# Rotating a matrix by 90 degrees: a staging grid of 63 places, three output buffers, and a late chunk

## The chip, the cores and the metric

The kernel runs on one core of one Trainium2 chip. The time is the device time of one execution in microseconds, and the number that counts is the median of several runs. A profile is one more execution, taken by the hardware profiler.

## The reference

```
def reference(x, k):            # x: 8192 x 8192 float32, k = 1
    return np.rot90(x, k)       # out[8191 - j, i] = x[i, j]
```

Every element is read once and written once: 268.44 MB in and 268.44 MB out. No arithmetic is done.

## The kernel before

**Tiles.** The matrix is cut into 16 tiles of 1024 rows by 4096 columns (`tiles`, line 71). A tile has T = 8 row tiles t of 128 rows, and its columns have 8 chunks c of C = 512. `grid` (line 63) holds one whole tile on chip, 8 x 8 places of 512 floats in each of the 128 partitions.

**A rotation in two halves.** A row tile is loaded in one DMA of 2 MB (128 partitions by 4096 floats) into a buffer `a` (line 92, issued by SP). `reverse` (line 96, VectorE, DVE in the profile) copies it into its 8 places of the grid, with each block of 128 columns in reverse order. `store` makes one output: TensorE (PE) transposes 32 blocks of 128x128, those of one chunk of all 8 row tiles, into two PSUM tiles of 2048 floats (line 119). ScalarE (ACT) copies each half to the output buffer `ot` (line 135) and issues one DMA of 2 MB to `out` (line 137).

**One grid for two tiles.** Output i of tile m reads one column of places, and when its transposes are done those 8 places are free. Row tile i of tile m+1 goes into them. So even tiles lie in the grid as (t, c) and odd ones as (c, t) (`row_tile`, line 75, and `block`, line 79). The order written out by hand (lines 145 to 155) is: load and reverse all of tile 0; then for each m and i: load row tile i of tile m+1, store output i of tile m, reverse row tile i of tile m+1. The last tile is stored in eight outputs of half the rows and twice the columns.

**Buffers.** `a_pool` and `o_pool` have two buffers each, of 16 KB in a partition; the grid has 128 KB. During the loads of tile 0, when nothing is stored yet, every third and fourth load borrows an output buffer (line 87). In the last tile three of the outputs borrow a load buffer (line 152).

**Who waits for whom.** A load waits until the reversal of the row tile that had its buffer is done. The reversal of row tile i waits for its load and for the transposes of output i. The transposes wait for ACT to empty PSUM. ACT's copy waits for the transposes and for the landing of the store that had the output buffer. The first output of a tile needs the last row tile; there the transposes run row tile by row tile (`by_row`), so that the last comes last.

Of the kernel before, what the change touches and what calls it, by code (L numbers as in the profile page):

```python
# [2 lines left out]

# [5 lines left out]

P = 128  # L10
T = 8
R = T * P
W = 4096
C = W // T
F = 4096
FP = 2048


def whole_reads(nc):

    for fn in nc.m.functions:
        for block in fn.blocks:
            for n, ins in enumerate(block.instructions):
                if not isinstance(ins, mybir.InstDMACopy):
                    continue
                src = ins.ins[0]
                ap = [list(d) for d in src.ap]
                if len(ap) == 3 and ap[2][0] == 1 and ap[1][0] == ap[2][1]:
                    ap = [ap[0], [1, 1], [1, ap[1][1] * ap[2][1]]]
                    block.instructions[n] = copy.replace(  # L30
                        ins,
                        ins=[copy.replace(src, ap=ap)],
                        ant_dge_precooked=False,
                    )


@with_exitstack
def kernel(
    ctx: ExitStack,
    tc: tile.TileContext,  # L40
    x: bass.AP,
    k: bass.AP,
    out: bass.AP,
):

    nc = tc.nc
    assert k == 1, f"only k=1 supported, got {k}"
    nc.at_finalize(whole_reads)

    N, M = x.shape
    dt = x.dtype

    consts = ctx.enter_context(tc.tile_pool(name="consts", bufs=1))  # L60
    ident = consts.tile([P, P], dt)
    make_identity(nc, ident)
    grid = consts.tile([P, T, T, C], dt)

    a_pool = ctx.enter_context(tc.tile_pool(name="a_pool", bufs=2))
    o_pool = ctx.enter_context(tc.tile_pool(name="o_pool", bufs=2))
    psum_pool = ctx.enter_context(
        tc.tile_pool(name="psum", bufs=2, space=bass.MemoryType.PSUM)
    )

    tiles = [(r0, c0) for r0 in range(0, N, R) for c0 in range(0, M, W)]
    LAST = len(tiles) - 1
    H = T // 2

    def row_tile(m, t):

        return grid[:, t] if m % 2 == 0 else grid[:, :, t]

    def block(m, t, b):

        c, b = divmod(b, C // P)
        at = grid[:, t, c] if m % 2 == 0 else grid[:, c, t]
        return at[:, b * P : (b + 1) * P]

    def load(m, t):
        r0, c0 = tiles[m]
        if m == 0 and t % 4 >= 2:
            a = o_pool.tile([P, W], dt, tag="o")
        else:
            a = a_pool.tile([P, W], dt, tag="a")  # L90
        r0 += t * P
        nc.sync.dma_start(out=a[:], in_=x[r0 : r0 + P, c0 : c0 + W])  # L92
        return a

    def reverse(m, t, a):
        nc.vector.tensor_copy(  # L96
            out=row_tile(m, t).rearrange("r c (b m) -> r c b m", m=P),
            in_=a[:].rearrange("r (c b m) -> r c b m", c=T, m=P)[:, :, :, ::-1],
        )

    def store(m, rows, i, pool, by_row):

        r0, c0 = tiles[m]
        r0 += rows[0] * P
        n = len(rows) * P
        G = F // n
        PW = FP // n
        if pool is a_pool:
            ot = a_pool.tile([P, F], dt, tag="a")
        else:  # L110
            ot = o_pool.tile([P, F], dt, tag="o")
        o = ot[:].rearrange("m (g f) -> m g f", g=G)
        ps = []
        for h in range(2):
            pt = psum_pool.tile([P, FP], mybir.dt.float32, tag="ps")
            ps.append(pt[:].rearrange("m (g f) -> m g f", g=PW))

        def transposes(h, w, t):
            nc.tensor.transpose(  # L119
                ps[h][:, PW - 1 - w, t * P : (t + 1) * P],  # L120
                block(m, rows[t], i * G + h * PW + w),
                ident,
            )

        if by_row:
            for t in range(len(rows)):
                for h in range(2):
                    for w in range(PW):
                        transposes(h, w, t)
        for h in range(2):  # L130
            if not by_row:
                for w in range(PW):
                    for t in range(len(rows)):
                        transposes(h, w, t)
            nc.scalar.copy(o[:, G - PW - h * PW : G - h * PW, :], ps[h])  # L135
        top = M - c0 - (i + 1) * G * P
        nc.scalar.dma_start(  # L137
            out=out[top : top + G * P, r0 : r0 + n].rearrange(
                "(g m) f -> m g f", g=G
            ),  # L140
            in_=o,
        )

    every = list(range(T))
    for t in every:
        reverse(0, t, load(0, t))
    for m in range(LAST):
        for i in every:
            a = load(m + 1, i)
            store(m, every, i, o_pool, i == 0)  # L150
            reverse(m + 1, i, a)
    pools = [o_pool, o_pool] + [a_pool, o_pool] * 3
    for i, pool in enumerate(pools):
        rows = every[i // H * H :][:H]
        store(LAST, rows, i % H, pool, False)


# [1 line left out]
_INS = ['x', 'k']  # L159
_OUTS = [((8192, 8192), 'float32')]  # L160

_NUMBERS = {'k': 1}


# [26 lines left out]
```

## Time and profile before

| | |
|---|---|
| three runs | 1267.73, 1269.55, 1270.55 us; median 1269.55 |
| the profiled execution | 1267.78 us, of which the span (first to last instruction) is 1265.9 us |
| DMA queue of the loads (q1), of the stores (q10) | 268.44 MB each; 49.7% and 50.0% of 16 engines' span |
| rate over the span | 424 GB/s |
| PE matmul | 721.7 us busy, 4096 instructions |
| ACT copies | 465.3 us busy, 256 of 1869 ns |
| DVE copies | 293.6 us busy, 128 of 2294 ns |
| a load, a store, from issue to landing (median) | 17.1 us, 15.9 us |
| what ends most of ACT's idle time | a store's landing: 733.5 us |
| what ends most of DVE's idle time | a load's landing: 717.5 us |

The profile page has the span in 40 slices with the busy share of each engine in tenths (9 is 90% or more) and the rate of the DMA engines, and the chain of work that ended last, followed back from the end. The trace answers further questions: the busy time of each engine in any stretch of the span (columns: stretch, its length, PE, PE's weight load, DVE, ACT and POOL busy with counts, the granted clock of PE, the mean busy share of the 16 DMA engines, GB/s), and instructions in order of time with the idle time before them and what ended it in square brackets. ACTq and SPq are the queues from which ACT and SP issue DMAs.

### The profile page before, as it was taken

The page shows a single profiled execution, that of the slowest core. Times are in us where ns is not written, and L with a number is a line of the kernel's source. Part 1 is how long each engine was busy: PE and PEld are TensorE (multiplying, and loading weights), DVE is VectorE, ACT ScalarE, POOL GpSimd, SP SyncE. Part 2 cuts the span into 40 slices and gives each one's busy share as a digit, 9 for nine tenths or more (in the row PEclk, how much of TensorE's full clock was granted, in tenths as well). Part 3 has the DMA queues.
Part 4 walks back from the last instruction along what each step waited for, and adds up shares of the span by engine and source line. Part 5 has one row for each costly group of instructions (what it writes and reads, how often), then busy time and mean ns, then how long its engine had stood idle before and what let it go on. Part 6 is the DMA issues. An engine that isn't in the chain of part 4 may idle for free.

```text
span 1265.9 us, 9281 instructions
## 1 busy us (share of the span) xinstructions
PE 721.7 (57%) x4096; PEld 683.4 (54%) x4096; DVE 293.6 (23%) x128; ACT 466.6 (37%) x257; POOL 0.7 (0%) x6
## 2 busy tenths in 40 slices
PE   1355665566556565565545655556565565565674
PEld 1355554556546554565545645556455564565574
DVE  3322222222222222222222222222222222222210
ACT  0243333433344333333343333433343333433364
POOL 0000000000000000000000000000000000000000
PEclk9977677676777868768687786877868768768687
DMA  9999999999999999999999999999999999999989
GB/s 398 428 427 426 427 429 430 430 428 429 428 430 430 429 429 429 428 430 428 429 429 429 430 428 429 428 429 427 427 429 428 429 427 426 429 427 428 429 361 375
DMA packets 36904, 537.48 MB, mean 425 GB/s; under 512 B 4096, under 2 KB 4096, under 8 KB 4096
## 3 DMA queue, kind: packets, MB, share of 16 engines
q10 hardware_dynamic: 18432, 268.44, 50.0%
q1 hardware_dynamic: 18432, 268.44, 49.7%
q8 instruction: 32, 0.52, 0.2%
q14 instruction: 8, 0.07, 0.0%
HBM read 268.44 MB, written 268.44 MB: 424 GB/s over the span
## 4 chain that ended last, share of the span: by engine, by line
DMA 78%; ACT 19%; issue 1%; DVE 0%; ACTq 0%; PE 0%; SPq 0%
DMA out_dram<-ot 75%; ACT ot L135 19%; DMA a<-in_x_dram 3%; DVE grid L96 0%; PE pt L119 0%; ACTq L137 0%; SPq L92 0%; ACTq L135 0%
## 5 line engine op out<-in xcount | busy, mean ns | idle before, releaser
L119 PE MATMUL pt<-ident,grid 128*128 128x128 f32 x4096 | 721.7, 358 | 528.2 <-ACT ot L135 491.2
L119 PEld LDWEIGHTS pt<-ident,grid 128*128 128x128 f32 x4096 | 683.4, 192 | 566.3 <-ACT ot L135 526.3
L135 ACT COPY ot<-pt 128x2048 f32<-128x2048 f32 x256 | 465.3, 1869 | 745.7 <-DMA out_dram<-ot 733.5
L96 DVE COPY grid<-a 128x4096 f32<-128x4096 f32 x128 | 293.6, 2294 | 920.7 <-DMA a<-in_x_dram 717.5
L135 ACT ACT_TABLE_LOAD x1 | 1.3, 1283 | 39.8 <-DVE grid L96 39.8
masks.py:199 POOL TENSOR_SCALAR_AFFINE_SELECT ident<-ident 128x128 f32<-128x128 f32 x1 | 0.3, 292 | 0.1
masks.py:197 POOL MEMSET ident<- 128x128 f32 x1 | 0.2, 204 | 0.3 <-POOLq L172 0.3
L172 POOL MEMSET const-bfloat16-1.0<- 128x1 bf16 x1 | 0.1, 101 | 0.0
L172 POOL MEMSET const-uint8-127<- 128x1 uint8 x1 | 0.1, 101 | 0.0
L172 POOL MEMSET const-float32-0.0<- 128x1 f32 x1 | 0.1, 98 | 0.2 <-issue 0.2
L172 POOL MEMSET const-float32-1.0<- 128x1 f32 x1 | 0.1, 98 | 0.0
## 6 DMA issues: line engine op xcount, KB each, us to landing
a<-in_x_dram SPq DMA_DIRECT2D x128, 2048.0 KB, 17.1
out_dram<-ot ACTq DMA_DIRECT2D x128, 2048.0 KB, 15.9
```

Of the source, the lines that this page charges most:

```text
L96: nc.vector.tensor_copy(out=row_tile(m, t).rearrange("r c (b m) -> r c b m", m=P), in_=a[:].rearrange("r (c b m) -> r c b m", c=T, m=P)[:, ...
L119: nc.tensor.transpose(ps[h][:, PW - 1 - w, t * P : (t + 1) * P], block(m, rows[t], i * G + h * PW + w), ident,)
L135: nc.scalar.copy(o[:, G - PW - h * PW : G - h * PW, :], ps[h])
L172: nc = _bacc.Bacc("TRN2", target_bir_lowering=False, num_devices=1)
```

## The change

The grid gets 63 places in place of 64 (126 KB), and `o_pool` three buffers in place of two. To do with one place fewer, chunk 0 of each row tile takes the place of the next row tile's chunk 0. Chunk 0 of the last row tile takes that of the first one, which must have been transposed by then, and the corner (7, 7) takes place 0. So `reverse` is done in parts: chunks 1 to 7 at once as before (`reverse_most`; for the last row tile chunks 1 to 6 and then 7), and chunk 0 one output later, after the next output's transposes, in front of the next row tile's chunks. For the last row tile of a tile, chunk 0 comes in the middle of the next tile's first output: after its row tile 0 was transposed, or, in the last tile, after the first half. The row tile's load buffer stays in use until then. In tile 0 the loads 2, 3, 4 and 7 borrow output buffers.

```
-    grid = consts.tile([P, T, T, C], dt)
+    grid = consts.tile([P, T * T - 1, C], dt)
...
-    o_pool = ctx.enter_context(tc.tile_pool(name="o_pool", bufs=2))
+    o_pool = ctx.enter_context(tc.tile_pool(name="o_pool", bufs=3))
...
-    def row_tile(m, t):
-
-        return grid[:, t] if m % 2 == 0 else grid[:, :, t]
+    def place(m, t, c):
+        if c == 0:
+            t, c = (t + 1, 0) if t < T - 1 else (1, 0)
+        elif t == c == T - 1:
+            t, c = 0, 0
+        return t * T + c if m % 2 == 0 else c * T + t
+
+    def places(m, t, c, n):
+
+        at = place(m, t, c)
+        step = 1 if m % 2 == 0 else T
+        return grid[:, at : at + (n - 1) * step + 1 : step]
...
-        if m == 0 and t % 4 >= 2:
+        if m == 0 and t % 5 >= 2:
...
-    def reverse(m, t, a):
+    def reverse(m, t, a, c, n):
         nc.vector.tensor_copy(
-            out=row_tile(m, t).rearrange("r c (b m) -> r c b m", m=P),
-            in_=a[:].rearrange("r (c b m) -> r c b m", c=T, m=P)[:, :, :, ::-1],
+            out=places(m, t, c, n).rearrange("r c (b m) -> r c b m", m=P),
+            in_=a[:, c * C : (c + n) * C].rearrange(
+                "r (c b m) -> r c b m", c=n, m=P
+            )[:, :, :, ::-1],
         )
...
+    def reverse_most(m, t, a):
+
+        if t < T - 1:
+            reverse(m, t, a, 1, T - 1)
+        else:
+            reverse(m, t, a, 1, T - 2)
+            reverse(m, t, a, T - 1, 1)
...
                 for h in range(2):
                     for w in range(PW):
                         transposes(h, w, t)
+                if waiting is not None and t == 0:
+                    reverse(m, T - 1, waiting, 0, 1)
         for h in range(2):
             if not by_row:
                 for w in range(PW):
                     for t in range(len(rows)):
                         transposes(h, w, t)
+                if waiting is not None and h == 0:
+                    reverse(m, T - 1, waiting, 0, 1)
             nc.scalar.copy(o[:, G - PW - h * PW : G - h * PW, :], ps[h])
...
     for t in every:
-        reverse(0, t, load(0, t))
+        a = load(0, t)
+        reverse_most(0, t, a)
+        if t < T - 1:
+            reverse(0, t, a, 0, 1)
+    waiting = a
     for m in range(LAST):
         for i in every:
             a = load(m + 1, i)
-            store(m, every, i, o_pool, i == 0)
-            reverse(m + 1, i, a)
+            store(m, every, i, o_pool, i == 0, waiting if i == 0 else None)
+            if i > 0:
+                reverse(m + 1, i - 1, waiting, 0, 1)
+            reverse_most(m + 1, i, a)
+            waiting = a
...
-        store(LAST, rows, i % H, pool, False)
+        store(LAST, rows, i % H, pool, False, waiting if i == 0 else None)
```

## The prediction

> **What bounds the kernel now.** I read three views, in this order. First the page's strip of 40 slices: is any engine full?
>
> ```profile
> PE   1355665566556565565545655556565565565674
> ...
> DMA  9999999999999999999999999999999999999989
> GB/s 398 428 427 426 427 429 430 430 428 429 428 430 430 429 429 429 428 430 428 429 429 429 430 428 429 428 429 427 427 429 428 429 427 426 429 427 428 429 361 375
> ```
>
> The DMA engines are full in every slice but the last two, at 426 to 430 GB/s; PE never passes seven tenths. The slices that lose rate are the first (398) and the last two (361, 375).
>
> Second the chain of waits as the page sums it:
>
> ```profile
> DMA 78%; ACT 19%; issue 1%; DVE 0%; ACTq 0%; PE 0%; SPq 0%
> ```
>
> It runs through landings of stores and the copies behind them. Taken alone that would promise a lot from another output buffer: 733.5 us of ACT's idle time ends on a store's landing. But the first view says that the DMA engines had other bytes to move in those waits, so they cost nothing while that holds. The question is where it does not hold.
>
> Third, therefore, the stretches view (DMA share is the column before the last, GB/s the last; the share reads 1.01 when all 16 engines are full, since neighbouring packets overlap a little):
>
> ```profile
> 62.00:1192.00 1130.00, 659.30 (x3680) 627.25 (x3680) 263.82 (x115) 417.97 (x230) 0.00 (x0) 0.75 1.01 428
> ...
> 1207.00:1209.00 2.00, 2.00 (x12) 2.00 (x11) 0.00 (x0) 0.19 (x1) 0.00 (x0) 0.50 0.58 246
> 1209.00:1213.00 4.00, 3.04 (x17) 2.80 (x15) 0.92 (x1) 0.80 (x1) 0.00 (x0) 0.71 1.05 446
> 1213.00:1214.00 1.00, 0.00 (x0) 0.00 (x0) 1.00 (x1) 1.00 (x2) 0.00 (x0) 1.00 0.39 164
> 1214.00:1216.00 2.00, 1.88 (x12) 1.88 (x13) 0.37 (x1) 1.84 (x2) 0.00 (x0) 0.69 0.12 49
> 1216.00:1217.00 1.00, 1.00 (x6) 1.00 (x5) 0.00 (x0) 0.00 (x0) 0.00 (x0) 0.50 0.00 0
> 1217.00:1221.00 4.00, 4.00 (x34) 4.00 (x32) 0.00 (x0) 3.33 (x2) 0.00 (x0) 0.85 1.08 459
> 1221.00:1223.00 2.00, 1.79 (x17) 1.55 (x16) 0.00 (x0) 0.79 (x2) 0.00 (x0) 1.00 0.62 262
> 1223.00:1263.00 40.00, 22.84 (x196) 20.94 (x194) 0.00 (x0) 25.08 (x14) 0.00 (x0) 0.87 0.99 412
> 1263.00:1266.00 3.00, 0.00 (x0) 0.00 (x0) 0.00 (x0) 0.00 (x0) 0.00 (x0) 0.50 0.05 22
> ```
>
> So the DMA engines have one hole, where the loads run out (the last is issued at 1194.3), and are full on both sides of it. Against 1.01 it loses 0.86 us in 1207:1209, 0.62 in 1213:1214, 1.78 in 1214:1216, 1.01 in 1216:1217 and 0.78 in 1221:1223, and 1209:1213 and 1217:1221 give back 0.16 and 0.28: **4.6 us**. The hole is not the same for all engines: a share of 0.12 in 1214:1216 is two of sixteen still busy. For those two only 1216:1217 and 1221:1223 are empty, 1.0 + 0.8 = **1.8 us**.
>
> **The change part by part.**
>
> *Third output buffer.* ACT's copy for output j now waits for the landing of store j-3 instead of j-2. In the hole, with the landings of the trace:
>
> ```profile
> 1203.56 3.63 ACT L135 COPY ot<-pt 128x2048 f32<-128x2048 f32 x2 [6.18 <-DMA out_dram<-ot]
> 1207.22 0.55 ACTq L137 DMA_DIRECT2D out_dram<-ot  x1
> 1212.20 3.63 ACT L135 COPY ot<-pt 128x2048 f32<-128x2048 f32 x2 [5.01 <-DMA out_dram<-ot]
> 1215.87 0.55 ACTq L137 DMA_DIRECT2D out_dram<-ot  x1
> ```
>
> The store issued at 1207.22 moves to the slot one landing earlier, 1197.4, and the one issued at 1215.87 to 1207.2; the next (now 1221.43) to about 1215.9. From issue to first bytes is some 1.5 us (issue 1215.87, DMA back after 1217). So the second has bytes ready by 1208.7, before the engines run dry at 1213, and feeds them for 4.9 us (2.097 MB at 428 GB/s), to about 1218; the third is ready by 1217.4. After that ACT delivers an output every 4.35 us (1222.61, 1227.00, 1231.31) and the DMA engines take 4.9 us for one, so the queue stays filled. The hole closes for all engines with at least a microsecond or so in hand. What is late next is the DMA work itself.
>
> How much of 4.6 us reaches the end depends on the slowest DMA engine, since the others' time in the hole was partly spent waiting for it. If the two late engines stay the last to the end, the gain is their own idle time, 1.8; if another is last (in 1263:1266 the share 0.05 is 2.4 engine-us, one or two engines that finish late after all were level again at 1223), it approaches 4.6. The trace does not say which. I take the middle, **-3.2 us**, ends -1.8 and -4.6.
>
> [...]
>
> *Reversal cut in two.* 112 row tiles get two copies on DVE and 16 (t=7) get three, so 272 instead of 128, with the same elements. 128x4096 takes 2294 ns; no smaller one is in the trace. The 144 added ones cost between nothing (bytes alone count) and 144 x 2.29 = 330 us of DVE. The nearest row for a tiny instruction, 98 to 101 ns for a 128x1 MEMSET on POOL, would make it 14 us. DVE is busy 293.6 of 1265.9 us and idle some 7.4 us of each 9.8 us output, so this hides in the wait for loads up to the far end (two whole copies are 4.6 of 9.8 us). Without that cover, 0.1 us an output. **0**. [...]
>
> *Row tile held one output longer.* The small copy of row tile i-1 goes ahead of row tile i's large copy on DVE; both wait for the same transposes of output i, so nothing new queues behind it there. But SP's load n into that buffer now waits for it. Around 604 us: store landing, ACT at 603.88, PE from 605.80 to 611.84 (8.0 us after), reversal 612.49 to 614.78 (10.9 after). Before, load n is issued 10.9 us after the landing of store n-5. After, PE is one output ahead thanks to the third buffer, and load n goes 8.0 + some 0.4 = 8.4 us after the same landing. The two shifts cancel, with 2.5 us to the good. **0** in steady state.
>
> *Order at a tile's first output.* In it PE does t=0, then DVE the held chunk (about a quarter to 0.4 us), while PE has t=1 to 6 to do (24 transposes, over 2 us at the granted clock); t=7 comes last. **0**. In the last tile the held chunk lies between the two halves of an output that reads rows 0 to 3 only, so nothing there waits for it.
>
> *Start.* Five loads instead of four may start at once; the DMA share is 1.00 from 2 to 42 us already. The load of (1,2) is issued after the transposes of output 1 (52.75) plus the small copy, at 53.2, instead of 49.7. Load (1,0) has landed by 47.37, load (1,1) follows 4.9 us later, and the store issued at 49.12 is another 4.9 us of work, so the engines are busy to about 57. **0**, at worst 1 us.
>
> *Sum.* The profiled execution is 1267.78, its span 1265.9 and 1.88 around it; minus 3.2 gives 1264.6. It is one of the quick ones: the median is 1269.55, 1.77 above. The forecast is for the median: 1269.55 - 3.2 = **1266.4 us**.
>
> **Rivals.**
>
> 1. *The slowest DMA engine was never idle enough.* Saving 1.8 or less: 1267.8 up to 1269.5, inside 0.2% (2.5 us, about what a measurement here can tell from no change). For it: 0.12 in 1214:1216. Against: all were level at 1223 and the lateness at the end arose later.
> 2. *The buffer's lead is eaten and the hole stays*: 1269.5. That needs ACT to wait for PE where it waited for stores. Against: ACT waits 12.2 us in all for PE, ten times.
> 3. *Slower: the tile boundary.* Place: output 0 of 14 tiles needs row tile 7 of its own. Load 7 leaves 8.4 us after store 2's landing, lands 17.1 (median) later, then 2.3 + 0.5 reversal and 0.7 transposes: 29.0. The copy may start at store 5's landing, 29.4. The cover is 0.4 us; before it was 39.2 - 31.0 = 8.2. It decides only when DMA runs dry: two stores queued are 9.8 us, less 5.2 for copy and first bytes, so 4.6 more, a load of over 22 us; the longest now is 20.7. Each us beyond costs 14: 1269.55 + 14 = 1283.6.
>
> **How the numbers follow.** Hole closed and 2.5 us or more saved: 0.52. Rival 1: 0.25. Rival 2: 0.12. Rival 3: 0.11. So faster 0.52, same 0.37, slower 0.11. The low end is the quickest run shown, 1267.73, less 4.6: 1263.1. The high end takes in no change at the slowest run, 1270.55, with a little of rival 3's foot: 1270.8.
>
> **What would show it.** Right: a DMA share near 1.0 from 1207 to 1223; the ACT issue spacing there under 5 us; the load issues still 9.8 us apart; 272 DVE copies, the small ones under 0.5 us. Wrong: shares under 0.9 every 78 us (eight outputs), which is rival 3; a hole of the same size, rival 2; no hole but an end in which a few engines run 3 us or longer past the rest, rival 1.

## The result, and the profile after

| | before | after |
|---|---|---|
| median of 15 runs | 1268.22 us (1267.02 to 1270.55) | 1266.01 us (1265.32 to 1266.68) |
| profiled execution, span | 1265.9 us | 1264.3 us |
| ratio after : before | | 0.9982, 95% interval 0.9974 to 0.9990 |

The changed kernel is 2.2 us faster, 0.18% (0.10 to 0.26%). The forecast was 3.2 us, from 1269.55 to 1266.4; with more runs the kernel before has a lower median.

The strip of the changed kernel, same rows as before:

```profile
PE   1545544655556554555445545455454665556663
...
DMA  9999999999999999999999999999999999999998
GB/s 399 415 431 429 429 429 428 431 428 430 428 428 429 430 428 429 429 429 429 428 430 431 427 430 428 429 430 428 429 429 429 422 427 429 429 428 422 429 412 351
```

The slice before the last, which lost rate before (361), now has 412. But the second slice has fallen from 428 to 415: something was lost at the start, where the kernel before lost nothing.

The stretches of the changed kernel around the old hole and the end (DMA share before the last column, GB/s last):

```profile
62.00:1192.00 1130.00, 608.87 (x3680) 565.69 (x3680) 369.25 (x244) 418.09 (x231) 0.00 (x0) 0.76 1.01 429
1207.00:1209.00 2.00, 1.21 (x12) 0.97 (x9) 2.00 (x1) 0.00 (x0) 0.00 (x0) 1.00 1.02 434
1209.00:1213.00 4.00, 0.05 (x1) 0.05 (x1) 1.47 (x2) 1.97 (x2) 0.00 (x0) 0.97 1.00 426
1213.00:1217.00 4.00, 4.00 (x23) 4.00 (x24) 0.98 (x1) 1.67 (x1) 0.00 (x0) 0.60 1.00 426
1217.00:1221.00 4.00, 1.81 (x17) 1.57 (x16) 1.45 (x3) 2.51 (x2) 0.00 (x0) 1.00 1.00 422
1221.00:1223.00 2.00, 2.00 (x20) 1.96 (x19) 0.00 (x0) 1.25 (x2) 0.00 (x0) 1.00 0.68 279
1223.00:1225.00 2.00, 1.34 (x13) 1.11 (x12) 0.00 (x0) 2.00 (x2) 0.00 (x0) 1.00 0.97 393
1225.00:1258.00 33.00, 18.49 (x160) 17.10 (x159) 0.00 (x0) 19.72 (x11) 0.00 (x0) 0.88 1.00 419
1258.00:1260.50 2.50, 0.00 (x0) 0.00 (x0) 0.00 (x0) 0.00 (x0) 0.00 (x0) 0.50 0.38 157
1260.50:1264.30 3.80, 0.00 (x0) 0.00 (x0) 0.00 (x0) 0.00 (x0) 0.00 (x0) 0.50 0.04 17
```

Of the 4.6 us some 0.7 are left, at 1221:1223. In exchange there is a new ragged end: from 1258 the share is 0.38, and after 1260.5 it is 0.04, less than one engine of sixteen. Before, the share was 0.99 up to 1263. So the engines' mean work ends earlier by over 3 us, but the last of them only 1.6 us earlier. The trace has 16 landings for each store, called its parts here. A part is taken as what one DMA engine moved: from 1261.2 to 1262.9 one part of the last store is still out, and the share is 0.07, some one engine of sixteen. The landings say the same: the 16 parts of the last store landed between 1263.0 and 1265.1 before, between 1258.6 and 1263.5 after.

ACT around the hole, in order of time, with what ended its waits:

```profile
1204.89 0.55 ACTq L162 DMA_DIRECT2D out_dram<-ot  x1
1211.03 3.64 ACT L160 COPY ot<-pt 128x2048 f32<-128x2048 f32 x2 [6.17 <-DMA out_dram<-ot]
1214.70 0.55 ACTq L162 DMA_DIRECT2D out_dram<-ot  x1
1218.49 3.64 ACT L160 COPY ot<-pt 128x2048 f32<-128x2048 f32 x2 [3.82 <-DMA out_dram<-ot]
1222.16 0.55 ACTq L162 DMA_DIRECT2D out_dram<-ot  x1
```

Seven stores go from 1222.16 to 1248.13, all but the first of the last tile's eight. So 1214.70 is that first one (1221.43 before), and 1204.89 is the store that went at 1215.87 before, 11 us earlier. The one of 1222.16 is late: its copy waited until 1218.4 for the slowest part of an older store.

The copies on DVE, by shape (busy and mean ns of one, then idle time ahead):

```profile
L107 DVE COPY grid<-a 128x3584 f32<-128x3584 f32 x112 | 331.1, 2957 | 709.2 <-DMA a<-in_x_dram 605.8 <-PE pt L140 103.4
L107 DVE COPY grid<-a 128x512 f32<-128x512 f32 x144 | 59.0, 419 | 1.6 <-PE pt L140 1.6
L107 DVE COPY grid<-a 128x3072 f32<-128x3072 f32 x16 | 28.2, 1760 | 100.1 <-DMA a<-in_x_dram 100.1
```

The small ones take 0.42 us. But seven chunks take longer on average than eight did (2957 ns against 2294).

### The profile page after: what moved, and what is told of

Read it like the earlier page. It is cut to its first block, busy times and chain, and to the rows that moved or that the text cites. A ratio compares the mean times of both kernels' runs of the same rounds, so it can differ in the third digit from the quotient of the medians.

```text
span 1264.3 us, 9438 instructions
## 1 busy us (share of the span) xinstructions
PE 670.5 (53%) x4096; PEld 621.0 (49%) x4096; DVE 407.6 (32%) x272; ACT 467.8 (37%) x257; POOL 0.7 (0%) x6
## 4 chain that ended last, share of the span: by engine, by line
DMA 78%; DVE 9%; ACT 6%; PE 2%; issue 2%; ACTq 0%; DVEq 0%; SPq 0%
DMA a<-in_x_dram 56%; DMA out_dram<-ot 23%; DVE grid L107 9%; ACT ot L160 6%; PE pt L140 2%; ACTq L162 0%; DVEq L107 0%; SPq L103 0%; ACTq L160 0%
## 5 line engine op out<-in xcount | busy, mean ns | idle before, releaser
L140 PE MATMUL pt<-ident,grid 128*128 128x128 f32 x4096 | 670.5, 338 | 575.3 <-ACT ot L160 404.8
L140 PEld LDWEIGHTS pt<-ident,grid 128*128 128x128 f32 x4096 | 621.0, 179 | 624.5 <-ACT ot L160 442.5
L107 DVE COPY grid<-a 128x512 f32<-128x512 f32 (+2 forms) x272 | 407.6, 1543 | 810.8 <-DMA a<-in_x_dram 705.9
```

The lines of the kernel that those rows point to most:

```text
L107: nc.vector.tensor_copy(out=places(m, t, c, n).rearrange("r c (b m) -> r c b m", m=P), in_=a[:, c * C : (c + n) * C].rearrange("r (c b m) ...
L140: nc.tensor.transpose(ps[h][:, PW - 1 - w, t * P : (t + 1) * P], block(m, rows[t], i * G + h * PW + w), ident,)
```

## The experiments

Theory A: the end is that DMA engine of the sixteen that has most to do. Theory B: a lost share counts for all engines alike. Times are medians. Each ratio is to the kernel before on the same chip; where two times come from different chips, the text says so.

### The change again

Its edit: none.

> The changed kernel itself, to have it on the same chip as the three that follow. Two theories are to be told apart. Theory A (slowest engine): the end is set by the one of the 16 DMA engines that has most to do, and the hole counted only as far as that engine idled in it; the engines differ because each of the 32 packets that fetch PE's code (queue q8) holds one engine for 1.0 to 1.4 us. Theory B (mean): each us of DMA share lost counts for all engines alike (4.6 us in the hole), and what is missing of it was given back in the middle, through the cut reversal (DVE 407.6 us busy for 293.6) and the row tile held longer. Both expect 2 to 2.5 us below the kernel before, a ratio near 0.998. A expects that the engines' last landings of the last store lie 4 to 5 us apart again.

Measured: 1266.04 us beside 1268.68 before, ratio 0.9978 (0.9969 to 0.9988). The last store landed between 1258.5 and 1263.4. The ragged end repeats, 4.9 us wide.

### Its first half alone: two output buffers

```
-    o_pool = ctx.enter_context(tc.tile_pool(name="o_pool", bufs=3))
+    o_pool = ctx.enter_context(tc.tile_pool(name="o_pool", bufs=2))
...
-        if m == 0 and t % 5 >= 2:
+        if m == 0 and t % 4 >= 2:
```

> The grid of 63 places and the late chunk, but two output buffers: the cost of the first half of the change by itself. Theory A: a load leaves 8.4 us after the landing of store n-4, 7.3 us later than before in its place, so some 0.75 of a load fewer is in flight (17.1 us from issue to landing becomes about 10); the engines still always have a store, so the DMA share stays at 1.01 in the middle and the time is that of the kernel before within 1.5 us, with the hole at the end. Theory B: what the third buffer's gain lost in the middle (2.4 us of 4.6) shows here openly: 2 to 3 us slower than before. A third outcome, if the held row tile is no free choice: DMA share under 1 at each output, 10 us or more slower.

Measured: 1268.25 us, ratio 0.9997 (0.9988 to 1.0006). The stretches of this run:

```profile
58.00:60.00 2.00, 0.61 (x6) 0.61 (x7) 0.00 (x0) 2.00 (x2) 0.00 (x0) 1.00 0.84 303
...
62.00:1192.00 1130.00, 659.30 (x3664) 624.57 (x3662) 369.26 (x244) 415.70 (x229) 0.00 (x0) 0.75 1.01 428
...
1213.00:1217.00 4.00, 4.00 (x21) 4.00 (x20) 0.61 (x1) 0.84 (x1) 0.00 (x0) 0.50 0.81 340
...
1220.00:1224.00 4.00, 3.74 (x32) 3.46 (x32) 0.00 (x0) 2.65 (x3) 0.00 (x0) 1.00 0.35 147
```

The middle is as full as ever and the hole stays, as 0.35 in 1220:1224. The late chunk, the cut reversal and loads that leave later (8.95 us after the landing of store n-4, against 1.20 before; medians of 90 loads) cost nothing in the middle. That part of theory B falls. The low rate at 58:60 belongs to this half of the change.

### The hole alone: load buffers for the late outputs

The kernel before with

```
-            store(m, every, i, o_pool, i == 0)
+            late = m == LAST - 1 and i == T - 1
+            store(m, every, i, a_pool if late else o_pool, i == 0)
...
-    pools = [o_pool, o_pool] + [a_pool, o_pool] * 3
+    pools = [o_pool, a_pool] * 4
```

> The kernel before, grid of 64 places, two output buffers, but the last output of the last tile but one uses a load buffer that is free by then, and the outputs of the last tile use the two pools in turn. Only the hole is touched: the store now issued at 1215.87 should go at about 1214 (the transposes end at 1212), the next before 1219. Theory A: the late engines' own idle time, 1.2 to 1.8 us, goes nearly whole: 1 to 2 us faster than before. Theory B: 2 to 3 us of the hole's mean go and nothing is given back in the middle: 2 to 3 us faster, at least as good as the change.

Measured: 1265.11 us, ratio 0.9972 (0.9960 to 0.9983), some 3.6 us faster than before (2.3 when it was run again, below), on that chip 0.9 us better than the change. The stretches, and ACT at the store in question:

```profile
1207.00:1209.00 2.00, 2.00 (x14) 2.00 (x13) 0.00 (x0) 0.23 (x2) 0.00 (x0) 0.65 0.79 336
1209.00:1213.00 4.00, 3.79 (x35) 3.50 (x33) 1.99 (x1) 3.47 (x2) 0.00 (x0) 1.00 0.99 418
1213.00:1217.00 4.00, 3.42 (x32) 3.15 (x31) 0.31 (x1) 3.64 (x2) 0.00 (x0) 1.00 0.96 406
1217.00:1221.00 4.00, 3.40 (x32) 3.17 (x31) 0.00 (x0) 3.53 (x2) 0.00 (x0) 1.00 0.98 410
1221.00:1223.00 2.00, 2.00 (x20) 1.85 (x18) 0.00 (x0) 1.33 (x2) 0.00 (x0) 1.00 0.97 401
```

```profile
1208.82 3.65 ACT L135 COPY ot<-pt 128x2048 f32<-128x2048 f32 x2 [1.77 <-DMA a<-in_x_dram]
1212.50 0.55 ACTq L137 DMA_DIRECT2D out_dram<-ot  x1
```

The hole is down to 0.9 us over these stretches. It went further than both theories had it: the store left at 1212.50, earlier than the 1214 reckoned, since its copy waited 1.77 us in place of 5.01 and no longer for a store's landing. A had expected 1 to 2 us, B 2 to 3; by the size alone B was nearer.

### Half of the transposes

```
-                for w in range(PW):
+                for w in range(PW // 2):
...
-            nc.scalar.copy(o[:, G - PW - h * PW : G - h * PW, :], ps[h])
+            for half in range(2):
+                top = G - PW - h * PW + half * (PW // 2)
+                nc.scalar.copy(
+                    o[:, top : top + PW // 2, :], ps[h][:, PW // 2 : PW, :]
+                )
```

> The changed kernel with half of the transposes left out (the output takes each of the others twice, so half of the blocks are not the reference's): same DMAs, same DVE work, the ACT copies cut in two. PE's code is half as long, so queue q8 should have 16 packets for 32. Theory A: the engines that are held are held twice instead of four times, 1.4 us each: 2 to 3 us faster than the changed kernel, though PE is on no path. Theory B: PE is not the bound and the bytes are the same: within 0.7 us of the changed kernel.

Measured: 1261.67 us, ratio 0.9940 (0.9927 to 0.9952), 4.4 us below the changed kernel on the same chip, though PE was idle half of the time anyway. The DMA queue that carries PE's code, in this run, in the changed kernel again, and in the run with half more transposes below:

```profile
q8 instruction: 16, 0.26, 0.1%
```

```profile
q8 instruction: 32, 0.52, 0.2%
```

```profile
q8 instruction: 48, 0.79, 0.2%
```

Each packet is 16 KB of code and takes some 1005 ns (median of the 32, before and after), where a packet of data, also of 16 KB, takes 611. That one engine is held four times by 32 packets was A's estimate: their times repeat every eight packets (in the kernel before 1006, 1009, 996, 1034, 1032, 1019, 949 and 949 ns from 532 to 808 us, then 1005, 1008, 994, 1033, 1034, 1022, 949 and 952), which would fit eight engines in turn, but the trace names no engine. The gain is more than A expected, and it is not at the late engine only: the first engine to finish ended 3.9 us earlier too (its part of the last store landed at 1254.5, against 1258.5). The edit halves PE's work along with its code, and makes 512 ACT copies of 256; so the run doesn't tell the fetch of the code from the work.

### The start mended: load (1,2) early

```
-        if m == 0 and t % 5 >= 2:
+        if (m == 0 and t % 5 >= 2) or (m == 1 and t == 0):
```

> The changed kernel, with row tile 0 of tile 1 also loaded into an output buffer, so that load (1,2) finds a load buffer free and goes at about 40 us instead of 53.2. Theory S (restart): between 52 and 56 us the changed kernel has no load in flight, and from 56 to 62 the load that restarts has slow packets (385, 270 and 410 GB/s at a DMA share of 1.0); that costs 1.0 us of all engines. It expects 427 GB/s there and 0.8 to 1.1 us less than the changed kernel. Rival: the place is early, the engines drift apart for another 1200 us, and what decides the end is the spread that the fetches make: within 0.3 us of the changed kernel.

The changed kernel in these stretches:

```profile
56.00:58.00 2.00, 1.42 (x14) 1.18 (x11) 1.75 (x2) 1.90 (x2) 0.00 (x0) 1.00 1.00 385
58.00:60.00 2.00, 1.98 (x18) 1.94 (x19) 0.00 (x0) 1.74 (x1) 0.00 (x0) 1.00 0.93 270
60.00:62.00 2.00, 1.76 (x16) 1.52 (x14) 0.00 (x0) 1.59 (x1) 0.00 (x0) 1.00 1.02 410
```

and with the load early:

```profile
56.00:58.00 2.00, 1.64 (x15) 1.40 (x13) 1.97 (x2) 1.62 (x1) 0.00 (x0) 1.00 0.98 418
58.00:60.00 2.00, 1.70 (x16) 1.70 (x16) 0.00 (x0) 2.00 (x2) 0.00 (x0) 1.00 0.93 393
60.00:62.00 2.00, 2.00 (x19) 1.76 (x17) 0.00 (x0) 0.01 (x1) 0.00 (x0) 1.00 1.05 442
```

A share near 1 with 270 GB/s is a place where a packet takes longer: the loads' packets between 56 and 60 take 770 ns on average, up to 1394, and 613 with the load early. (No packet of a load runs for 4.4 us ahead of this stretch, and for 4.7 us in the run with two output buffers, which loses rate here too. In the run with the load early there is a pause of 2.1 us from 59.8, and the packets behind it take 612 ns.) Against 428 the changed kernel loses 2 x 43 + 2 x 158 + 2 x 18 = 438 KB, 1.0 us. The whole run: 1265.61 us, ratio 0.9983 (0.9974 to 0.9992), beside the 1266.01 and 1266.04 of the changed kernel on two other chips, and 0.5 us below the next run, on the same chip. So some half of the 1.0 us reached the end: between the theory and its rival.

### The rest of the hole

The changed kernel with

```
-    pools = [o_pool, o_pool] + [a_pool, o_pool] * 3
+    pools = [a_pool, o_pool] * 3 + [o_pool, a_pool]
```

> The changed kernel, with the first output of the last tile in a load buffer, so that its copy does not wait for the landing at 1218.4 and the rest of the hole (0.68 at 1221:1223 and 0.97 after it) goes. Theory A (slowest engine): the late engines have no gap there, the fast ones 1 to 2 us: the end stays within 0.3 us of the changed kernel. Theory B (mean): 0.6 to 0.8 us faster.

Measured: 1266.14 us, ratio 0.9983 (0.9974 to 0.9992), no gain over the changed kernel on its two other chips (0.9982 and 0.9978). The stretch where the share was 0.68:

```profile
1221.00:1223.00 2.00, 1.79 (x17) 1.55 (x15) 0.00 (x0) 1.30 (x2) 0.00 (x0) 1.00 0.89 369
```

It was filled by 0.4 us and bought nothing; instead the last store's landings lie 5.5 us apart (4.9 before the edit). Engines that were early are earlier. That is what theory A expects.

### Half more transposes

```
-            nc.tensor.transpose(
-                ps[h][:, PW - 1 - w, t * P : (t + 1) * P],
-                block(m, rows[t], i * G + h * PW + w),
-                ident,
-            )
+            for again in range(2 if w % 2 == 0 else 1):
+                nc.tensor.transpose(
+                    ps[h][:, PW - 1 - w, t * P : (t + 1) * P],
+                    block(m, rows[t], i * G + h * PW + w),
+                    ident,
+                )
```

> The changed kernel with half of the transposes made twice (the same values into the same place): PE has 6144 matmuls, its code takes 48 packets on q8 for 32, and the bytes of loads and stores are the same. PE then works some 7 of each 9.8 us. By the run with half of the transposes (4.4 us less for 16 packets fewer) the theory that the fetch of code is what costs expects 3.5 to 5 us more than the changed kernel, the DMA share staying at 1.01. A theory by which only waits count expects nothing up to 64 us, or, if PE becomes the bound, DMA shares under 0.95 in the middle and tens of us more.

Measured: 1271.54 us, ratio 1.0028 (1.0016 to 1.0039), 5.4 us above the run before it on the same chip. The DMA share stays at 1.01 in the middle:

```profile
62.00:1205.00 1143.00, 781.91 (x5602) 749.55 (x5601) 374.01 (x246) 424.86 (x233) 0.00 (x0) 0.83 1.01 427
1226.00:1230.00 4.00, 4.00 (x39) 4.00 (x38) 0.00 (x0) 2.82 (x2) 0.00 (x0) 1.00 0.53 217
```

In the tail PE now sets a pace of 5.25 us an output, and a hole of 0.53 comes back at 1226:1230. It is not what the run lost: the last landings come 5.05 us apart there instead of 5.01, over seven stores 0.3 us, and were 5.5 us behind those of the changed kernel run again already at 1211 (1.9 at 160, 3.7 at 650). So the loss grows over the whole run, and about 5.1 us are left for 16 packets of code more and half more of PE's work. With 16 packets and half of the work gone it was 4.4 us. That is 0.27 to 0.32 us at the end for each packet of code and the work that goes with it, both ways.

### Both mends together

The edits of the two sections on the start and on the rest of the hole, and

```
-        if t < T - 1:
-            reverse(m, t, a, 1, T - 1)
-        else:
-            reverse(m, t, a, 1, T - 2)
-            reverse(m, t, a, T - 1, 1)
+        reverse(m, t, a, 1, T - 2)
+        reverse(m, t, a, T - 1, 1)
```

> The changed kernel with both edits of the two runs before (load (1,2) early, the first output of the last tile in a load buffer), and the reversal of chunks 1 to 7 always cut into 1 to 6 and 7. The cut should bring the DVE busy time from 407.6 us to some 330, since 128x3072 takes 1760 ns on average and 128x3584 2957; that is worth nothing at the end in either theory, DVE being idle two thirds of the time. Theory A with S: 1.0 us less than the changed kernel, 1265.0. Theory B with S: 1.7 us less, 1264.3.

Measured: 1265.34 us, ratio 0.9979 (0.9971 to 0.9988), 0.7 us below the changed kernel on its two chips and 0.8 below the run on the rest of the hole on the same chip. The stretches of its end:

```profile
1225.00:1254.00 29.00, 16.77 (x128) 15.52 (x128) 0.00 (x0) 17.00 (x10) 0.00 (x0) 0.81 1.00 418
1254.00:1259.00 5.00, 0.00 (x0) 0.00 (x0) 0.00 (x0) 0.00 (x0) 0.00 (x0) 0.50 0.57 236
1259.00:1263.60 4.60, 0.00 (x0) 0.00 (x0) 0.00 (x0) 0.00 (x0) 0.00 (x0) 0.50 0.04 18
```

The first parts of the last store land at 1254.6, 8.4 us earlier than in the kernel before, and the last at 1262.7, 2.4 us earlier. One engine alone is at work after 1259.4 (0.04 of 16 engines over 4.6 us is 3 us of one). Everything that the edits gave to the others is idle time now. DVE is busy 311.4 us.

### Which engine is late

best1 with the last store cut by partitions:

```
+        for n in [8, 9, 10, 11, 12, 13, 14, 15, 15, 14, 7] if last else [P]:
+            nc.scalar.dma_start(out=to[p : p + n], in_=o[p : p + n])
+            p += n
```

> The run best1, with the last store cut into eleven, of 8 to 15 partitions and again 15, 14 and 7, to see which DMA engines take part in each and whether the one late engine is among them. In the runs before, one engine lands the last store 2.4 to 3.3 us after the second to last. If it is an engine that the narrow stores use, their last landings are as late as that of the wide store ahead of them; if it is one that they leave out, the narrow ones land 3 us or more earlier than the late engine. The time itself is no aim here: engines that take part in all eleven get more work, and the end should be up to 2 us later or 3 us earlier than best1 accordingly.

Measured: a single run, 1271.29 us; an issue took ACT 1.6 us, so the eleven were fed slowly, and the time says nothing of the engines. The landings do. Of the wide store ahead, 15 parts landed by 1254.9 and one at 1259.1. The store of eight partitions landed in eight parts, seven of them by 1254.9 and one at 1259.8; in those of 9, 10 and 11 partitions too one part came 4.0 to 4.9 us after the one before it. So, a part taken as one engine's, the late engine is one of the eight that this store used. Which eight of the sixteen those are no run shows; narrower stores were not tried for it.

### The two candidates side by side

> The run tail_only again, on one chip with best1, to see whether the grid of 63 places and the third output buffer are needed at all. Theory A: all that the change can win is the late engines' wait in the hole, and one load buffer at the end wins it too, without a loss at the start: 1265.1, the same as best1 within 0.5 us and 0.7 to 1 us below the changed kernel's 1266.0. Rival: its first result was luck of that chip, and the third buffer is worth 0.5 us or more beyond it: 1265.8 or later.

> The run best1 again, beside tail_again: 1265.3, with 15 engines done by 1259 and one alone at 1262 to 1263. If the late engine is always one of the same, its lag repeats within 1 us of 3.3; if it was chance, the lag differs.

Measured: the hole alone 1265.40 us, ratio 0.9980 (0.9971 to 0.9989); both mends 1265.32 us, 0.9982 (0.9973 to 0.9991). They are equal. They are 0.6 us below the changed kernel's 1266.0 on two other chips, but not by the ratio to the kernel before (0.9982 and 0.9978 there). The late engine landed 2.9 us after the second in best1 this time, 3.3 us the first time. The edit of the last outputs' buffers in the kernel before gets as much as the new grid and the third buffer.

## Why the prediction was right or wrong

**The number.** That 1266.4 lies 0.4 us from the measured 1266.01 is partly luck. The median that the forecast started from, 1269.55 of three runs, was 1.3 us above that of fifteen, and the saving was 1.0 us less than the 3.2 forecast.

**The hole closes: right.** 4.6 us to 0.7. The store of 1215.87 was forecast for 1207.2 and went at 1204.89, the next for 1215.9 and went at 1214.70. The third, due at some 1220.3 by the forecast pace of 4.35 us, went at 1222.16, after the slowest part of an older store: the rest of the hole.

**How much of it reaches the end: the size near, the reason not.** The prediction took the middle of 1.8 (only the late engines' idle time counts) and 4.6 (the mean), without a ground for a middle. The runs say that the engine which lands last counts, as in rival 1: filling the rest of the hole bought nothing (1266.14), in best1 fifteen engines ended 3.3 us or more before the last, and the sign that rival 1 named, an end in which few engines run on, came, if by 2.4 us past the next engine and not by 3. The last landings of the stores show what that came to. All loads are in by 1216, and from the last landing of the tenth store from the end nine stores are left in both kernels. Before, they took 48.0 us (1217.07 to 1265.08). In the changed kernel they took 45.1 (1218.42 to 1263.50, and as long when it was run again), one every 5.01 us without a gap. The hole alone agrees, with 45.2 and 44.8 us. So the tail gave 2.9 us, more than rival 1's bound and near the middle, but for a reason that the prediction did not have. In the kernel before, the last landings lie 5.5, 6.3 and 6.2 us apart from 1217 to 1235. Against 5.0, the first two are 1.8 us of waiting, as reckoned for the late engines. The third is no waiting: a packet of code runs from 1228.3 to 1229.2, and one part of a store then lands 1.9 us after the other fifteen, which were level.

The prediction held against rival 1 that all engines were level at 1223. They were: the parts of one store landed between 1222.35 and 1222.54. But it was the hole that levelled them, since the early ones waited in it. Two stores earlier the parts lay between 1207.2 and 1212.1, and in the changed kernel, where nothing had levelled them, between 1199.8 and 1211.0. There the packets of code at 1222.7 and 1242.7 did not delay the last landings, which kept their 5.0 us.

**Start: the term that was mis-sized.** It was put at "0, at worst 1 us", because stores would keep the engines busy. They were busy (share 1.03 from 52 to 56). But with no load in flight from 52 to 56 us, the load that follows had slow packets (770 ns on average): 1.0 us of rate, 0.5 us at the end. With -2.9 for the tail and +0.5 for the start the sum is -2.4; measured is -2.2, the interval of the ratio being -3.3 to -1.3. By the last landing of the tenth store from the end the changed kernel is 1.2 to 1.4 us behind the kernel before (1218.26 and 1218.42 against 1217.07), with the load early 0.6 us (1217.63). How much of that is scatter is not shown: the hole alone, run twice, has 1217.04 and 1218.52 there.

**The row tile held longer: the price right, the way there not.** Two buffers with the late chunk are within 0.1% of before, and the middle stays at 1.01. But the two shifts did not cancel: load n was to leave 8.4 us after the landing of store n-5, in place of 10.9, and leaves 17.3 us after it (median of 90 loads). The thin cover at a tile's first output showed: ACT waits 257.1 us for PE in 44 places (12.2 before). All this cost the DMA engines almost nothing, with loads still queued: rival 3 did not come.

**Cut reversal: hidden, as said, but dearer than the nearest row.** By the row of 98 to 101 ns DVE would have been busy 308 us, by the far end 624; measured is 407.6. Seven chunks side by side take 2.03 us, seven chunks eight places apart 3.89 (below). The 14 us for 144 more instructions, from the same row, was low as well: six, seven and eight chunks side by side take 1.76, 2.03 and 2.29 us, 0.27 a chunk, which as an estimate leaves 0.16 us fixed in each instruction, some 23 us in all. Cutting seven into six and one took 96 us off DVE, and best1's time fits without a gain from it; alone it was not run.

**What stays open.** Why a code packet, with its share of PE's work, costs 0.27 to 0.32 us at the end is not settled. In the traces each one is followed within 25 ns by a data packet of 1.02 us (median) in place of 0.61, so it takes some 1.4 us of its engine, if the packet behind it is on the same one. If the 16 packets went to 16 engines in turn, that would be 1.4 us for each engine, to eight in turn 2.8; which engines they go to, and how often to the late one, no run shows. PE's work itself is the rival. Between 62 and 1190 us the data packets far from any code packet (those that don't run from 2 us before one to 4 us after it) took 613.1, 613.6 and 614.6 ns on average with half, all and half more of the transposes (613.4 in the first profile of the changed kernel). Over the 2048 data packets of an engine that is, as an estimate, 1.0 and 2.0 us, so part of the 4.4 and 5.4 us seems to come without the code. No run changes the code alone. Which engine is late, and why that one, is open as well: the last part of a store lands 0.3 us after the second last at 300 us and 2.8 us after it at 1200 in the changed kernel run again.

## What to carry to other kernels

The DMA share of 1.01 was a mean here over sixteen engines that drifted apart (in the changed kernel run again the last part of a store landed 0.3 us after the second last at 300 us, 2.8 at 1200): before pricing a hole, see which engines idle in it, and after closing it, look at how ragged the end is. Work on an engine with time to spare had its price here, though the transfers were the bound: half of PE's transposes left out was worth twice the whole change (4.4 us against 2.2), by the fetch of their code through the DMA engines, by the work itself or by both. And a hole at one place may be filled at that place: load buffers borrowed for the last outputs did here what a new layout of the grid did (ratios 0.9972 and 0.9980 against 0.9982 and 0.9978).

## What the runs showed of the hardware that was not expected

- Code: 32 packets of 16 KB for 8192 PE instructions, some 1005 ns each on one engine, and the data packet behind each takes 1.02 us in place of 0.61. 16 packets and half of the transposes fewer: -4.4 us; 16 packets and half of the transposes more: +5.4 us.
- A load that started after 4.4 us without one in flight had packets of 770 ns on average instead of 611, at a DMA share of 0.93 to 1.02; behind a pause of 2.1 us they took 612. Whether the pause is the cause no run shows apart from the rest.
- The reversing copy on DVE, in order of time, two kinds of tile next to each other (start, us for both copies of a row tile or three of the last):

```profile
655.19 2.36 DVE L107 COPY grid<-a 128x3584 f32<-128x3584 f32 x2 [7.50 <-DMA a<-in_x_dram]
664.97 2.43 DVE L107 COPY grid<-a 128x3072 f32<-128x3072 f32 x3 [7.42 <-DMA a<-in_x_dram]
674.83 4.22 DVE L107 COPY grid<-a 128x3584 f32<-128x3584 f32 x2 [7.43 <-DMA a<-in_x_dram]
```

The trace has 2027 ns for the seven chunks of 512 where the places lie side by side and 3886 where they are eight apart (the rows above join copies that overlap a little). Eight chunks took 2.29 us in both layouts before, and six take 1.76 in both. So of six, seven and eight only seven with a step were slow, at half the speed; other odd counts were not run.
